# Scattering the gates of two steps at a time, with the low-gate one-hots scaled on ScalarE

## The chip, the cores and the metric

The kernel runs on one core of a Trainium2 chip. The metric is device time in microseconds (us), taken as the median of the timed runs. A profiled execution of the same program gives the traces that are quoted.

## What is computed

A trunk of two layers, 256 tokens of width 1024. Each layer has a token mixer (mLSTM in the first, RG-LRU in the second) with memory cross-attention, and then a PEER channel mixer. The change is in the PEER mixer:

```python
def peer_ffn(x, w_q, subkeys, u_tab, v_tab):      # PEER_EXPERTS = 128 * 128, 8 heads, top 16
    ...
        q = (xb @ w_q).reshape(n, PEER_HEADS, 2, PEER_HALF)
        s = jnp.einsum('nhpc,pkc->nhpk', q, sk)
        sv, si = lax.top_k(s, PEER_TOPK)
        cand = sv[:, :, 0, :, None] + sv[:, :, 1, None, :]
        cand_id = si[:, :, 0, :, None] * PEER_KEYS + si[:, :, 1, None, :]
        fv, fi = lax.top_k(cand.reshape(n, PEER_HEADS, PEER_TOPK * PEER_TOPK), PEER_TOPK)
        eid = ...                                  # the chosen experts, 8 * 16 = 128 for each token
        gw = jax.nn.softmax(fv, axis=-1)           # and their gates
        act = jax.nn.gelu(jnp.einsum('nhkd,nd->nhk', u_tab[eid], xb), approximate=False)
        return jnp.einsum('nhk,nhkd->nd', gw * act, v_tab[eid])
```

## The kernel before

The PEER mixer gathers nothing. It runs through all 128 x 128 experts in 128 blocks of 128, block i holding the experts whose number has one fixed second key. A step of the first half of the mixer computes `u @ x` for one block and all 256 tokens (`u_step`, 24 matmuls into one bank of the accumulator memory). The gates of the chosen experts are brought into the same layout, and products of gates and gelu values then weight the rows of `v` in the second half.

One core works in fp32 with each operand split into a high and a low part. For each block that is loaded (`next`, which calls `pump`), ScalarE casts the raw 128x1024 tile to the high part (L96), and VectorE and GpSimd subtract to get the low part. In the stage that the change touches, VectorE does columns 384 to 1023 (L104) and GpSimd the first 386 (L106); two columns are written by both, so that GpSimd starts behind VectorE. `u_step` of block i prepares block i + 2: three buffers (`HL_BUFS`) hold the two parts, so the cast for block i + 2 waits until TensorE is done with block i - 1. All engines execute their instructions in the order in which the program lists them.

A layer's `u` blocks are done in two stages. In the first (64 blocks, `lo`), VectorE also does the routing. In the second (63 blocks, `hi`; one more follows it), each step also scatters the gates of four tokens:

- `onehots(j)` builds, for the four tokens of step j, fp16 one-hot rows `oh`: VectorE compares an iota with the first and second key numbers (L878, 1024 elements a partition), then multiplies the first-key one-hots by the gates, which are held as a high and a low fp16 part (`gT`): both products are one instruction, L881, 1024 elements a partition, and the low product overwrites the one-hots it is made from.
- `scatter` is eight 128-column matmuls on TensorE (L1011) from `oh` into one bank: the gate of each expert for the four tokens.
- `finish(j)` applies gelu to the bank that `u_step(j)` left (`gated`: L911 and L913 on ScalarE, then the product L914 on VectorE), and brings the scattered gates in: a copy L902 on ScalarE, products L903 and L905 on VectorE.

The second stage lists, in step j: `u_step(j)`, `scatter` for step j, `finish(j - 1)`, `onehots(j + 1)`. `oh` has two buffers. [...]

Of the kernel before, what the change touches and what calls it, by code (L numbers as in the profile page):

```python
# [7 lines left out]
F32 = mybir.dt.float32  # L8
# [4 lines left out]
AF = mybir.ActivationFunctionType  # L13
ALU = mybir.AluOpType
# [3 lines left out]
P = 128  # L18
D = 1024
T = 256  # L20
# [23 lines left out]
class Trunk:  # L44
# [751 lines left out]
    def routing(self, w, tt):  # L796
        nc = self.nc
        sv, si, tmp = self.sv[tt], self.si[tt], self.tmp
        self.pool_cols = D
        sf = w.tile([P, 8, 2, 16], F16, name="sf")  # L800
        nc.vector.tensor_copy(sf, si)
        yield 0.4
        cand = w.tile([P, 8, NCAND], F32, name="cand")
        for n, (a0, na, nb, o) in enumerate(CAND):
            dv = cand[:, :, o:o + na * nb].rearrange("p h (a b) -> p h a b", a=na)
            i0 = sv[:, :, 0, a0:a0 + na].unsqueeze(3).to_broadcast([P, 8, na, nb])
            i1 = sv[:, :, 1, 0:nb].unsqueeze(2).to_broadcast([P, 8, na, nb])
            nc.vector.tensor_add(dv, i0, i1)
        yield 1.5
        fv = w.tile([P, 8, 16], F32, name="fv")  # L810
        fi = w.tile([P, 8, 16], U32, name="fidx")
        for h in range(0, 8, 2):
            yield from self.top16(*[(cand[:, h + p, :], fv[:, h + p, :], fi[:, h + p, :], tmp[:, p, :NCAND])
                                    for p in range(2)])
        self.pool_cols = 0
        gw = w.tile([P, 8, 16], F32, name="gw")
        gsum = w.tile([P, 8], F32, name="gsum")
        nc.vector.tensor_sub(gw, fv, fv[:, :, 0:1].to_broadcast([P, 8, 16]))
        nc.scalar.activation(gw, gw, AF.Exp)
        ff = w.tile([P, P], F16, name="ff")  # L820
        nc.vector.tensor_copy(ff, fi.rearrange("p a b -> p (a b)"))
        yield 0.6

        ge = w.tile([P, 2, 8, P], F16, name="ge")
        ab = w.tile([P, 2, P], F16, name="ab")
        over = w.tile([P, P], F16, name="over")
        nc.vector.tensor_tensor(ge[:, 0], self.edge, ff.unsqueeze(1).to_broadcast([P, 8, P]), op=ALU.is_le)
        nc.vector.tensor_scalar(over, ff, -float(TAIL0), 0.0, op0=ALU.add, op1=ALU.max)
        nc.vector.tensor_mul(ge[:, 1], ge[:, 0], self.wide)
        yield 1.7  # L830
        for n in (4, 2):
            nc.vector.tensor_add(ge[:, :, 0:n], ge[:, :, 0:n], ge[:, :, n:2 * n])
        nc.vector.tensor_add(ab, ge[:, :, 0], ge[:, :, 1])
        nc.vector.tensor_add(ab, ab, over.unsqueeze(1).to_broadcast([P, 2, P]))
        nc.vector.tensor_sub(ab[:, 1], ff, ab[:, 1])
        yield 1.9
        ef = w.tile([P, 2, P], F32, name="ef")
        for z in range(2):
            eq = w.tile([P, 8, 16, 16], F16, name="eq")
            full = [P, 8, 16, 16]  # L840
            nc.vector.tensor_tensor(eq, self.iotac.unsqueeze(1).to_broadcast(full),
                                    ab[:, z].rearrange("p (h k) -> p h k", h=8).unsqueeze(2).to_broadcast(full),
                                    op=ALU.is_equal)
            yield 1.25
            for hs in (slice(0, 4), slice(4, 8)):
                nc.vector.tensor_mul(eq[:, hs], eq[:, hs], sf[:, hs, z, :].unsqueeze(3).to_broadcast([P, 4, 16, 16]))
                yield 1.25
            for n in (8, 4, 2):
                nc.vector.tensor_add(eq[:, :, 0:n], eq[:, :, 0:n], eq[:, :, n:2 * n])
            nc.vector.tensor_add(ef[:, 1 - z].rearrange("p (h k) -> p h k", h=8), eq[:, :, 0], eq[:, :, 1])  # L850
            yield 1.8
        nc.vector.tensor_reduce(gsum, gw, axis=AX.X, op=ALU.add)
        nc.vector.reciprocal(gsum, gsum)
        nc.vector.tensor_mul(gw, gw, gsum.unsqueeze(2).to_broadcast([P, 8, 16]))
        yield 0.9

        def done():
            p = self.bank()
            n = P // 4
            js = slice(tt * n, (tt + 1) * n)  # L860
            steps = lambda a: a.rearrange("p (j t) -> p j t", t=4)
            nc.tensor.transpose(p[:, 0:P], ef[:, 0, :], self.ident)
            nc.tensor.transpose(p[:, P:2 * P], ef[:, 1, :], self.ident)
            nc.tensor.transpose(p[:, 2 * P:3 * P], gw.rearrange("p a b -> p (a b)"), self.ident)
            for z in range(2):
                nc.vector.tensor_copy(self.i12T[:, js, z], steps(p[:, z * P:(z + 1) * P]))
            gs = w.tile([P, n, 4], F32, name="gs")
            nc.vector.tensor_scalar(gs, steps(p[:, 2 * P:3 * P]), GSCALE, None, op0=ALU.mult)
            nc.vector.tensor_copy(self.gT[:, js, 0], gs)
            nc.vector.tensor_sub(self.gT[:, js, 1], gs, self.gT[:, js, 0])  # L870
        self.ready = done

    def onehots(self, j):
        nc = self.nc
        oh = self.ohp.tile([P, 3, 2, P, 2], F16, name="oh")
        pairs = lambda a: a.rearrange("p z (q t) -> p (z q) t", t=2).unsqueeze(2).to_broadcast([P, 4, P, 2])
        flat = lambda a: a.rearrange("p z q e t -> p (z q) e t")
        nc.vector.tensor_tensor(flat(oh[:, 1:3]), self.iota2.unsqueeze(1).to_broadcast([P, 4, P, 2]),  # L878
                                pairs(self.i12T[:, j]), op=ALU.is_equal)
        two = oh[:, 1].rearrange("p q e t -> p (q e t)").unsqueeze(1).to_broadcast([P, 2, 4 * P])  # L880
        nc.vector.tensor_tensor(flat(oh[:, 0:2]), two.rearrange("p z (q e t) -> p z q e t", q=2, t=2), pairs(self.gT[:, j]), op=ALU.mult)  # L881
        return oh

    def u_step(self):
# [31 lines left out]
    def peer_layer(self, layer):  # L916
        nc, tc, A = self.nc, self.tc, self.A
        with ExitStack() as ctx:
            wg = ctx.enter_context(tc.tile_pool(name=f"wglo{layer}", bufs=1))
            self.i12T = wg.tile([P, T // 4, 2, 4], F16, name="i12T")  # L920
            self.gT = wg.tile([P, T // 4, 2, 4], F16, name="gT")
            right = ctx.enter_context(ExitStack())
            lo = right.enter_context(tc.tile_pool(name=f"lo{layer}", bufs=1, side="right")).tile([P, N0, T], F32,
                                                                                               name="wglo")
            self.pool_cols = POOL_COLS
            with ExitStack() as rctx:
# [52 lines left out]
                for gq in range(2):  # L979
                    qb = self.proj_t(8, (self.xH, self.xL))  # L980
                    for b in range(4):
                        o = 8 * gq + 2 * b
# [8 lines left out]
                prev = None  # L991
                for i in range(N0 + 1):
                    g = self.u_step() if i < N0 else None
                    if prev is not None:
                        nc.scalar.activation(lo[:, i - 1, :], prev, AF.Gelu)
                    prev = g
                self.finish_sides()
            hi_p = ctx.enter_context(tc.tile_pool(name=f"wghi{layer}", bufs=1))
            hi = hi_p.tile([P, P - N0, T], F32, name="wghi")
            nj = P - N0  # L1000
            self.pool_cols, self.chained = HALF_COLS, True
            with ExitStack() as octx:
                self.ohp = octx.enter_context(tc.tile_pool(name=f"oh{layer}", bufs=2))
                oh = self.onehots(0)
                prev = None
                def scatter():
                    wp = self.bank()
                    for q in range(4):
                        qs = slice(q * P, (q + 1) * P)
                        for z in (0, 1):  # L1010
                            nc.tensor.matmul(wp[:, qs], oh[:, 2, q // 2, :, q % 2], oh[:, z, q // 2, :, q % 2], start=z == 0,  # L1011
                                             stop=z == 1, skip_group_check=True)
                    return wp
                for j in range(nj - 1):
                    g = self.u_step()
                    wp = scatter()
                    if prev is not None:
                        self.finish(lo, hi, j - 1, *prev)
                    if j == nj - 2:
                        oh = self.onehots(j + 1)  # L1020
                    prev = (g, wp)
                    if j < nj - 2:
                        oh = self.onehots(j + 1)
                wp = scatter()
                self.finish(lo, hi, nj - 2, *prev)
                self.finish(lo, hi, nj - 1, None, wp)
            cp = ctx.enter_context(tc.tile_pool(name=f"cp{layer}", bufs=HL_BUFS))
            cp.tile([P, GAP], F32, name="gap", bufs=1)
            self.pool_cols, self.chained = 0, False
# [7 lines left out]
            g = self.u_step()  # L1037
# [185 lines left out]
```

## Time and profile before

| | |
|---|---|
| median of three runs | 1867.91 us |
| lowest and highest | 1865.24 us, 1870.0 us |
| profiled execution, its own time | 1865.7 us |
| profiled execution, span | 1863.9 us |
| granted TensorE clock over the span | 0.99 |
| TensorE busy, VectorE busy, ScalarE busy, GpSimd busy | 98%, 70%, 50%, 23% |
| stage with the scatter, first to last scatter, first layer | 386.09 us to 589.82 us |
| matmuls and weight loads of the scatter | 1024 of each, in two layers |

In the rows below PE is TensorE's matmuls, PEld its weight loads, DVE VectorE, ACT ScalarE, POOL GpSimd. A row of the timeline holds the start and the duration in us, the engine, the source line, the operation, and what it writes and reads; brackets at the end hold the idle time of the engine before it and what ended that. A row of the groups holds the count, the busy time in us and the mean of one in ns. A busy TensorE is not one at its peak, since matmuls overlap: the distance between starts tells more than the durations.

### The profile page before, as it was taken

How to read it: one execution, taken by the hardware profiler on the slowest of the kernel's cores; microseconds unless marked ns; L12 is line 12 of the kernel's file. 1: busy time of each engine (PE TensorE's matmuls, PEld its weight loads, DVE VectorE, ACT ScalarE, POOL GpSimd, SP SyncE). 2: the span in 40 equal slices, each digit the busy share in tenths (PEclk: the TensorE clock that was granted, in tenths of full speed). 3: DMA queues.
4: the chain of work that ended last, by engine and by line, in shares of the span. 5: the costliest groups of instructions: out<-in, count | busy, mean ns of one | idle time of the engine just before them, and what ended most of it. 6: DMA issues, size and time to landing. Idle time of an engine off the chain costs nothing.

```text
span 1863.9 us, 33272 instructions
## 1 busy us (share of the span) xinstructions
PE 1821.8 (98%) x12770; PEld 1675.5 (90%) x12770; DVE 1298.0 (70%) x2665; ACT 940.3 (50%) x1604; POOL 428.7 (23%) x326
## 2 busy tenths in 40 slices
PE   8999999999999999999998899999999999999997
PEld 8898999999999888888887699999999988888886
DVE  6474579689998555666556638695999975555556
ACT  5454555455545444555537255554555454555543
POOL 2005772343331000000010258425333300000001
PEclk9999999999999999999999899999999999999999
DMA  7465556655555666667644166666555566666664
GB/s 244 132 178 171 179 177 191 199 174 161 165 163 162 196 195 193 193 215 227 205 169 139 59 193 177 198 192 192 160 161 165 162 179 193 193 193 194 193 194 132
DMA packets 94344, 333.42 MB, mean 179 GB/s; under 512 B 10600, under 2 KB 12904, under 8 KB 93928
## 3 DMA queue, kind: packets, MB, share of 16 engines
q1 hardware_dynamic: 93320, 328.66, 58.3%
q10 hardware_dynamic: 864, 2.62, 0.4%
q8 instruction: 100, 1.64, 0.4%
q14 instruction: 60, 0.49, 0.1%
HBM read 330.19 MB, written 1.05 MB: 178 GB/s over the span
## 4 chain that ended last, share of the span: by engine, by line
PE 72%; issue 15%; POOL 7%; DVE 3%; ACT 1%; DMA 1%; SPq 0%; POOLq 0%; ACTq 0%; DVEq 0%
PE bank L164 23%; PE bank L165 23%; PE bank L163 23%; POOL wL L106 7%; PE bank L222 3%; DVE wL L111 1%; DMA raw<-in_w0kg_dram 1%; ACT wH L96 0%; DMA raw<-in_w0qx_dram 0%; DVE xc L700 0%; PE bank L314 0%; DVE aa L747 0%; DVE x L293 0%; POOL wL L109 0%; DVE x L288 0%
## 5 line engine op out<-in xcount | busy, mean ns | idle before, releaser
L96 ACT CAST wH<-raw 128x1024 fp32r<-128x1024 f32 (+2 forms) x608 | 632.3, 1041 | 791.0 <-PE bank L165 330.2
L111 DVE TENSOR_TENSOR wL<-raw,wH 128x1024 fp32r<-128x1024 f32 (+3 forms) x413 | 468.5, 1137 | 455.7 <-ACT wH L96 455.1
L163 PE MATMUL bank<-xHL,wH 128*128 128x256 f32 x2536 | 717.6, 283 | 5.9 <-ACT wH L96 4.5
L165 PE MATMUL bank<-xHL,wL 128*128 128x256 f32 x2536 | 704.5, 278 | 7.3 <-DVE wL L111 7.3
L164 PE MATMUL bank<-xHL,wH 128*128 128x256 f32 x2536 | 704.5, 278 | 0.2
L165 PEld LDWEIGHTS bank<-xHL,wL 128*128 128x128 f32 x2536 | 479.1, 189 | 9.3 <-DVE wL L111 9.1
L163 PEld LDWEIGHTS bank<-xHL,wH 128*128 128x128 f32 x2536 | 479.1, 189 | 6.6 <-ACT wH L96 4.5
L164 PEld LDWEIGHTS bank<-xHL,wH 128*128 128x128 f32 x2536 | 479.6, 189 | 0.9 <-DVE xHL L219 0.9
L165 PE MATMUL bank<-wH,cL 128*128 128x512 f32 x1024 | 398.4, 389 | 0.0
L164 PE MATMUL bank<-wL,cH 128*128 128x512 f32 x1024 | 398.3, 389 | 0.0
L163 PE MATMUL bank<-wH,cH 128*128 128x512 f32 x1024 | 398.3, 389 | 0.0
L109 POOL TENSOR_TENSOR wL<-raw,wH 128x1024 fp32r<-128x1024 f32 (+1 forms) x121 | 258.1, 2136 | 211.7 <-ACT wH L96 181.1
L165 PEld LDWEIGHTS bank<-wH,cL 128*128 128x128 f32 x1024 | 192.2, 188 | 40.0
L163 PEld LDWEIGHTS bank<-wH,cH 128*128 128x128 f32 x1024 | 192.2, 188 | 39.9
L164 PEld LDWEIGHTS bank<-wL,cH 128*128 128x128 f32 x1024 | 192.2, 188 | 39.8
L106 POOL TENSOR_TENSOR wL<-raw,wH 128x386 fp32r<-128x386 f32 x126 | 129.7, 1029 | 279.9 <-DVE wL L104 279.9
L303 POOL TENSOR_TENSOR x<-x,raw 128x256 f32<-128x256 f32 x7 | 5.3, 760 | 614.4 <-ACT x L300 614.4
L878 DVE TENSOR_TENSOR oh<-iota,i12T 128x1024 f16<-128x1024 f16 x128 | 130.5, 1020 | 0.0
L104 DVE TENSOR_TENSOR wL<-raw,wH 128x640 fp32r<-128x640 f32 x126 | 104.0, 825 | 7.4
L881 DVE TENSOR_TENSOR oh<-oh,gT 128x1024 f16<-128x1024 f16 x128 | 90.1, 704 | 4.4
L1011 PE MATMUL bank<-oh 128*128 128x128 f16 x1024 | 81.1, 220 | 1.1 <-DVE oh L881 1.1
L1011 PEld LDWEIGHTS <-oh 128*128 128x128 f16 x1024 | 58.9, 98 | 6.0 <-DVE oh L881 1.5
(269 smaller groups left out, 1524.1 us busy)
## 6 DMA issues: line engine op xcount, KB each, us to landing
raw<-in_u_dram SPq DMA_DIRECT2D x256, 512.0 KB, 3.7
raw<-in_v_dram SPq DMA_DIRECT2D x256, 512.0 KB, 4.3
raw<-in_w_q_dram SPq DMA_DIRECT2D x32, 512.0 KB, 3.7
raw<-in_w_out_dram SPq DMA_DIRECT2D x16, 512.0 KB, 4.5
raw<-in_w0qx_dram SPq DMA_DIRECT2D x8, 512.0 KB, 4.7
raw<-in_wkv_dram SPq DMA_DIRECT2D x8, 512.0 KB, 4.7
raw<-in_w1x_dram SPq DMA_DIRECT2D x8, 512.0 KB, 4.4
raw<-in_w0v_dram SPq DMA_DIRECT2D x8, 384.0 KB, 3.7
```

The source lines that it names most:

```text
L96: (nc.vector.tensor_copy if self.cast_dve else nc.scalar.copy)(h[:, c], r[:, c])
L104: nc.vector.tensor_sub(l[:, k:], r[:, k:], h[:, k:].bitcast(F32))
L106: nc.gpsimd.tensor_sub(l[:, :k], r[:, :k], h[:, :k].bitcast(F32))
L109: nc.gpsimd.tensor_sub(l[:, :k], r[:, :k], h[:, :k].bitcast(F32))
L111: nc.vector.tensor_sub(l[:, k:], r[:, k:], h[:, k:].bitcast(F32))
L163: mm(out, sH, mH, start=start, stop=False, skip_group_check=True)
L164: mm(out, sH, mL, start=False, stop=False, skip_group_check=True)
L165: mm(out, sL, mH, start=False, stop=stop, skip_group_check=True)
L222: self.nc.tensor.matmul(out, lhsT, rhs, start=start, stop=stop, skip_group_check=True)
L878: nc.vector.tensor_tensor(flat(oh[:, 1:3]), self.iota2.unsqueeze(1).to_broadcast([P, 4, P, 2]), pairs(self.i12T[:, j]), op=ALU.is_equal)
L881: nc.vector.tensor_tensor(flat(oh[:, 0:2]), two.rearrange("p z (q e t) -> p z q e t", q=2, t=2), pairs(self.gT[:, j]), op=ALU.mult)
L1011: nc.tensor.matmul(wp[:, qs], oh[:, 2, q // 2, :, q % 2], oh[:, z, q // 2, :, q % 2], start=z == 0, stop=z == 1, skip_group_check=True)
```

## The change

Three things change. The steps are taken in pairs: after the `u_step` of an odd step, the gates of both steps are scattered, 16 matmuls in a row, so both buffers of `oh` are filled before TensorE reads either. The product with the low part of the gates leaves VectorE, whose L881 now makes the high product alone (512 elements a partition); ScalarE makes the low product in place, with four activations of 128 columns, one for each token, which take the gate as a per-partition scale from a new fp32 copy `gL` (one more VectorE copy for each half of the tokens). And `finish` moves behind `onehots`: step j lists `u_step(j)`, `onehots(j)`, `finish(j - 2)`, and, if j is odd, the two scatters.

```diff
+            nc.vector.tensor_copy(self.gL[:, js], self.gT[:, js, 1])
...
-        two = oh[:, 1].rearrange("p q e t -> p (q e t)").unsqueeze(1).to_broadcast([P, 2, 4 * P])
-        nc.vector.tensor_tensor(flat(oh[:, 0:2]), two.rearrange("p z (q e t) -> p z q e t", q=2, t=2), pairs(self.gT[:, j]), op=ALU.mult)
+        nc.vector.tensor_tensor(oh[:, 0], oh[:, 1],
+                                self.gT[:, j, 0].rearrange("p (q t) -> p q t", t=2).unsqueeze(2)
+                                .to_broadcast([P, 2, P, 2]), op=ALU.mult)
+        for q in range(4):
+            one = oh[:, 1, q // 2, :, q % 2]
+            nc.scalar.activation(one, one, AF.Identity, scale=self.gL[:, j, q:q + 1])
...
-                for j in range(nj - 1):
-                    g = self.u_step()
-                    wp = scatter()
-                    if prev is not None:
-                        self.finish(lo, hi, j - 1, *prev)
-                    if j == nj - 2:
-                        oh = self.onehots(j + 1)
-                    prev = (g, wp)
-                    if j < nj - 2:
-                        oh = self.onehots(j + 1)
-                wp = scatter()
-                self.finish(lo, hi, nj - 2, *prev)
-                self.finish(lo, hi, nj - 1, None, wp)
+                ohs, gs, done = [self.onehots(0)], [], []
+                for j in range(nj):
+                    gs.append(self.u_step() if j < nj - 1 else None)
+                    if j:
+                        ohs.append(self.onehots(j))
+                    if done:
+                        self.finish(lo, hi, j - 2, *done.pop(0))
+                    if j % 2:
+                        done = [(g, scatter(o)) for g, o in zip(gs, ohs)]
+                        ohs, gs = [], []
+                for j in (nj - 2, nj - 1):
+                    self.finish(lo, hi, j, *done.pop(0))
```

More of the change, by code (lines that the diff above doesn't have):

```diff
@@ L921, in peer_layer @@
             self.gT = wg.tile([P, T // 4, 2, 4], F16, name="gT")
+            self.gL = wg.tile([P, T // 4, 4], F32, name="gL")
             right = ctx.enter_context(ExitStack())
@@ L1003, in peer_layer, with scatter @@
                 self.ohp = octx.enter_context(tc.tile_pool(name=f"oh{layer}", bufs=2))
-                oh = self.onehots(0)
-                prev = None
-                def scatter():
+                def scatter(oh):
                     wp = self.bank()
@@ L1010, in scatter @@
                         for z in (0, 1):
-                            nc.tensor.matmul(wp[:, qs], oh[:, 2, q // 2, :, q % 2], oh[:, z, q // 2, :, q % 2], start=z == 0,
-                                             stop=z == 1, skip_group_check=True)
-                    return wp
-                for j in range(nj - 1):
-                    g = self.u_step()
-                    wp = scatter()
-                    if prev is not None:
-                        self.finish(lo, hi, j - 1, *prev)
-                    if j == nj - 2:
-                        oh = self.onehots(j + 1)
-                    prev = (g, wp)
-                    if j < nj - 2:
-                        oh = self.onehots(j + 1)
-                wp = scatter()
-                self.finish(lo, hi, nj - 2, *prev)
-                self.finish(lo, hi, nj - 1, None, wp)
+                            nc.tensor.matmul(wp[:, qs], oh[:, 2, q // 2, :, q % 2], oh[:, z, q // 2, :, q % 2],
+                                             start=z == 0, stop=z == 1, skip_group_check=True)
+                    return wp
+                ohs, gs, done = [self.onehots(0)], [], []
[10 more added lines that the diff above has]
+                    self.finish(lo, hi, j, *done.pop(0))
             cp = ctx.enter_context(tc.tile_pool(name=f"cp{layer}", bufs=HL_BUFS))
```

## The prediction

> **What bounds the kernel now.** I read the page first, then the table by stage, then the timeline of one round of the touched stage, engine by engine.
>
> ```profile
> span 1863.9 us, 33272 instructions
> PE 1821.8 (98%) x12770; PEld 1675.5 (90%) x12770; DVE 1298.0 (70%) x2665; ACT 940.3 (50%) x1604; POOL 428.7 (23%) x326
> ...
> 460.00:500.00 40.00, 40.00 (x394) 39.57 (x393) 38.80 (x76) 20.16 (x48) 13.00 (x13) 1.00 0.54 165
> ```
>
> The page says TensorE. The third row (length; busy time of PE, PEld, DVE, ACT, POOL; clock; DMA share) says that in this stage VectorE is nearly as full, 38.80 of 40 us, and ScalarE half empty. The timeline shows who waits.
>
> ```profile
> 471.02 0.63 PE L1011 MATMUL bank<-oh 128*128 128x128 f16 x8
> 471.46 0.37 PE L163 MATMUL bank<-xHL,wH 128*128 128x256 f32 x1
> 471.66 0.28 PE L164 MATMUL bank<-xHL,wH 128*128 128x256 f32 x1
> 471.78 0.28 PE L165 MATMUL bank<-xHL,wL 128*128 128x256 f32 x1
> ...
> 474.29 0.63 PE L1011 MATMUL bank<-oh 128*128 128x128 f16 x8
> ...
> 472.23 0.83 DVE L104 TENSOR_TENSOR wL<-raw,wH 128x640 fp32r<-128x640 f32 x1
> 472.97 0.26 DVE L914 TENSOR_TENSOR wghi<-wghi,bank 128x104 f32<-128x104 f32 x1
> 473.14 0.42 DVE L903 SCALAR_TENSOR_TENSOR wglo<-bank,wglo 128x256 f32<-128x256 f32 x1
> 473.48 0.26 DVE L905 SCALAR_TENSOR_TENSOR wghi<-bank,wghi 128x108 f32<-128x108 f32 x1
> 473.65 1.05 DVE L878 TENSOR_TENSOR oh<-iota,i12T 128x1024 f16<-128x1024 f16 x1
> 474.74 0.69 DVE L881 TENSOR_TENSOR oh<-oh,gT 128x1024 f16<-128x1024 f16 x1
> 475.50 0.83 DVE L104 TENSOR_TENSOR wL<-raw,wH 128x640 fp32r<-128x640 f32 x1
> ...
> 471.15 1.05 ACT L96 CAST wH<-raw 128x1024 fp32r<-128x1024 f32 x1 [1.54 <-POOL wL L106]
> 472.10 0.29 ACT L911 ACTIVATE wghi<-bank 128x152 f32<-128x152 f32 x1
> 472.42 0.24 ACT L913 ACTIVATE bank<-bank 128x104 f32<-128x104 f32 x1
> 472.58 0.29 ACT L902 ACTIVATE wghi<-bank 128x148 f32<-128x148 f32 x1
> 474.41 1.05 ACT L96 CAST wH<-raw 128x1024 fp32r<-128x1024 f32 x1 [1.55 <-POOL wL L106]
> ```
>
> A round takes 3.27 us on every engine (471.02 to 474.29; 472.23 to 475.50). TensorE has no idle time in it: the eight matmuls of the scatter and the switch back take 471.02 to 471.66, then matmuls follow every 0.11 us. VectorE is full to some 0.07 us, ScalarE has 1.5 us free. The important thing is how this fits: ScalarE's gelu work (L911 to L902) runs while VectorE is in L104, so L914 finds its input ready. The two engines work side by side, with a cast ahead of both.
>
> **The change, part by part.** The grouped scatter saves TensorE a switch: the first matmul behind a scatter is 0.20 us from its follower (471.46, 471.66) where 0.12 is usual, so about 0.1 us for every second step, 6 us in all if TensorE stays the bound.
>
> The product on VectorE halves; this is the row for a fp16 product of 512 elements. Its neighbour here changes too. In the old order three products on fp32 lay between L104 and L878; now L878 follows L104 at once, while GpSimd runs L106. The first round of the stage has that order already:
>
> ```profile
> L849 DVE TENSOR_TENSOR eq<-eq 128x512 f16<-128x512 f16 x8 | 3.4, 426 | 0.3
> ...
> 384.92 0.82 DVE L104 TENSOR_TENSOR wL<-raw,wH 128x640 fp32r<-128x640 f32 x1
> 385.67 0.68 DVE L878 TENSOR_TENSOR oh<-iota,i12T 128x1024 f16<-128x1024 f16 x1
> 386.38 1.39 DVE L881 TENSOR_TENSOR oh<-oh,gT 128x1024 f16<-128x1024 f16 x1
> ...
> 385.83 1.40 POOL L106 TENSOR_TENSOR wL<-raw,wH 128x386 fp32r<-128x386 f32 x1 [2.12 <-DVE wL L104]
> ```
>
> L106 stretches to 1.40 us and L881 from 0.69 to 1.39: fp16 work on VectorE and GpSimd's subtraction shut each other out, and L881 ends 0.54 us behind L106 (387.77, 387.23), that is 0.15 less than its length alone. With 0.43 instead of 0.69 the new product ends 0.28 behind, at 387.51, 1.84 us after L878 began. Without the collision it would be 0.71 + 0.43 = 1.14. I take 1.84, since the row is this very order; 1.14 stays as an end of the range. VectorE's one-hots thus take no less time than now (473.65 to 475.43, 1.78).
>
> The four products on ScalarE have no row of their own. The nearest are back-to-back activations with a per-partition scale, of 256 columns, and two casts for the price of a column:
>
> ```profile
> 1018.40 0.49 ACT L737 ACTIVATE th<-rr,n 128x256 f32<-128x256 f32 x1
> 1018.79 0.49 ACT L736 ACTIVATE aa<-rr,c 128x256 f32<-128x256 f32 x1
> ...
> L96 ACT CAST wH<-raw 128x1024 fp32r<-128x1024 f32 x574 | 604.1, 1054 | 756.1 <-PE bank L165 320.5 <-POOL wL L106 187.5 <-PE bank L164 122.6
> L218 ACT CAST cH<-wglo 128x256 fp32r<-128x256 f32 x128 | 51.5, 404 | 1.0 <-DVE wglo L903 1.0
> ...
> 751.06 1.05 ACT L96 CAST wH<-raw 128x1024 fp32r<-128x1024 f32 x1 [1.36 <-PE bank L165]
> ...
> 752.14 1.22 DVE L111 TENSOR_TENSOR wL<-raw,wH 128x1024 fp32r<-128x1024 f32 x1 [1.16 <-ACT wH L96]
> ```
>
> A column costs (1054 - 404) / 768 = 0.85 ns, 128 columns less are 0.11 us, so one takes 0.38 us and they start 0.39 - 0.11 = 0.28 to 0.30 apart, say 0.29: four hold ScalarE for 1.17 us. Ends: 0.64, at the 0.16 us between L913 and L902, which have no scale operand; 1.7, if each waits for the one before (0.38 + 0.04, four times). The last two rows give the 0.04 us by which VectorE starts behind a cast that it waits for (752.11, 752.14); I use it in both directions.
>
> The speed is not the trouble. The trouble is the queue. In each step ScalarE now lists cast, four products, L911, L913, L902. The products overwrite what the VectorE product reads, so they wait for it; gelu, the copy and the next cast are queued behind them; and VectorE's L914, L903 and L905, listed behind the one-hots, wait for gelu. What ran side by side becomes one chain, counted from the start of a cast:
>
> - cast and hand-over: 1.09 (751.06 to 752.14)
> - L104 until L878 starts: 0.75 (384.92 to 385.67), so 1.84
> - L878 and the product: 1.84, so 3.68, and 0.04 to ScalarE, 3.72
> - four products until L911 starts: 1.17, so 4.89
> - L911 to L913 0.32, to L902 0.16, to the next cast 0.19 (0.29 less the 0.10 by which a follower starts early, 471.15 + 1.05 against 472.10): 0.67, so 5.56.
>
> VectorE waits for gelu at 4.89 + 0.32 + 0.24 + 0.04 = 5.49, and its three products (0.17, 0.34, 0.17 between starts) end at 6.2; the next L104 comes at 5.56 + 1.09 = 6.65, so they are hidden. TensorE needs 48 matmuls and two scatters for two rounds, 2 x 3.27 - 0.1 = 6.44 us against 11.12: it now waits, 4.7 us in each pair, at the scatter for ScalarE's products. All its other demands are met earlier: a block is prepared two rounds ahead, and L878 of a new pair, which overwrites what the scatter reads, comes 2.4 us after the last product ended, the scatter some 1.1.
>
> Per layer: in the trace the first cast is at 383.84 us and the last scatter here:
>
> ```profile
> 383.84 1.05 ACT L96 CAST wH<-raw 128x1024 fp32r<-128x1024 f32 x1
> ...
> 589.82 0.63 PE L1011 MATMUL bank<-oh 128*128 128x128 f16 x8 [0.57 <-DVE oh L881]
> ```
>
> The products of step 0 push that cast to about 385.9; step 0 has no one-hots behind it (1.0) and step 1 no `finish` (5.0), so step 2 begins at 391.9. Then 61 rounds of 5.56 lead to 731.1, and step 63, without a cast, needs some 3.5 more to its scatter: 734.6, against 589.82, 144.8 later. Two layers: 290. On the profiled execution's own 1865.7 us (span 1863.9 and 1.8 around it) that is 2156; the median of the runs shown, 1867.91, lies 2.2 above it, so 2158.
>
> [...]
>
> **The rivals.**
>
> TensorE stays the bound (not slower). If the chain were under 3.2 us, the 0.1 us for each pair would be left: 63 x 0.1 = 6 less, 1862. It needs gelu to start ahead of the products, as if `finish` stood first in the queue; then VectorE would need 0.75 + 1.84 + 0.68 = 3.27, just on the edge. Against it: the orders L96, L911, L913, L902 and L104, L914, L903, L905, L878, L881 in the rows above are the program's, so nothing reorders. 4 in 100.
>
> The overlap is lost in part: the products come out near 0.64 and the collision is missed. 5.56 - 0.53 - 0.70 = 4.33, 122 rounds of 1.06 more, 1998. Each end alone gives 2093 and 2073. Between 1900 and 2070: 6 in 100.
>
> TensorE's clock drops in the 4.7 us pauses. The one long pause of the trace:
>
> ```profile
> 1023.41 6.74 PE L222 MATMUL bank<-pT,vm 128*128 128x256 f32 x16 [5.87 <-ACT pT L66]
> ...
> 1023.40:1025.00 1.60, 1.59 (x4) 1.32 (x5) 1.59 (x3) 0.44 (x1) 0.00 (x0) 0.50 0.00 0
> 1029.00:1031.00 2.00, 2.00 (x9) 1.59 (x9) 0.41 (x1) 0.80 (x2) 0.00 (x0) 0.86 0.00 0
> 1031.00:1036.00 5.00, 4.71 (x27) 3.93 (x25) 2.36 (x6) 2.44 (x2) 0.00 (x0) 1.00 0.00 0
> ```
>
> After 5.87 us the granted clock is 0.50, and back at 1.00 some 6.2 us into the work. The scatter and the first block of a pair (0.97 + 2.72) would then end 6.8 us after the pause, where the second cast of the pair could start at 6.1 (0.58 + 5.56): 0.7 late, 63 pairs, 44 us, 2202 if it happens in every pair. 8 in 100. [...]
>
> A table load for each change between gelu and the scaling.
>
> ```profile
> L995 ACT ACT_TABLE_LOAD x6 | 7.7, 1283 | 0.1
> ...
> L300 ACT ACTIVATE x<-x,nm,rs 128x256 f32<-128x256 f32 x3 | 1.8, 597 | 2.6 <-DVE nm L328 2.6
> ```
>
> At 1.28 us twice a round it would give about 2470. But the loads belong to functions such as gelu (L995); L300, the same function as the products, has a row for its activations and none for a load. 2 in 100.
>
> **How the numbers follow.** The serial chain at its own size has 80 in 100. Its bounds: 2073 without the collision, 2158 + 0.5 x 122 = 2219 with each product waiting for the one before, and 2232 for the clock (44) with two of those waits in four (30). So 2070 to 2230, forecast 2158. A measurement of this kernel tells 0.3% (5.6 us) from no change: slower 0.95, faster 0.04, within 0.01.
>
> **What would show it.** Casts 5.56 us apart in the stage, the first layer's last scatter near 735 us. TensorE about 58% busy there, waiting some 4.7 us in each pair at L1011 for ScalarE's products. VectorE waiting about 1.8 us a round at L914 for L913, and ScalarE about 2.6 us a round for VectorE's product. That product near 1.1 us and L106 at 1.40; the four products 0.38 us each and 0.29 apart. It is wrong if gelu stands ahead of the products in ScalarE's order, if casts stay 3.2 us apart, or if TensorE has no idle time there; the size is wrong if the product ends 1.1 us behind L878's start, or the products are 0.16 or 0.42 apart.

## The result, and the profile after

The changed kernel took 2156.12 us (median of five runs, 2155.01 to 2156.47) against 1866.88 us for the kernel before (five runs too, of which the table above has the first three), a ratio of 1.1546 (95% interval 1.1529 to 1.1563). The forecast was 2158, range 2070 to 2230. The profiled execution took 2156.47 us, 290.8 more than the one before.

The profile's page and the waits of the changed kernel. In the page's second row of digits stands the granted clock.

```profile
span 2154.7 us, 33848 instructions
...
PE 1957.7 (91%) x12770; PEld 1772.9 (82%) x12770; DVE 1326.8 (62%) x2669; ACT 1086.8 (50%) x2116; POOL 472.2 (22%) x326
...
PEclk9999999888888999999999999998888889999999
...
ACT oh L886 <- DVE oh L881: 314.4, 119, 3.5
DVE wghi L919 <- ACT bank L918: 223.5, 122, 1.9
...
PE bank L1015 <- DVE oh L881: 141.5, 65, 3.6
```

Two waits are new and face each other: ScalarE's products (L886) wait for VectorE's product (L881), 314 us in all, and VectorE's gelu product (now L919) waits for ScalarE's gelu (now L918), 224 us in 122 steps. TensorE, which had waited for VectorE's product at the scatter for 1.1 us in all (the row below is of the kernel before), waits there (now L1015) for 141.5 us.

```profile
L1011 PE MATMUL bank<-oh 128*128 128x128 f16 x1024 | 81.1, 220 | 1.1 <-DVE oh L881 1.1
```

One round in the timeline, by engine; the comparison L878 is now L879, the copy L902 now L907:

```profile
550.77 1.05 ACT L96 CAST wH<-raw 128x1024 fp32r<-128x1024 f32 x1
554.53 1.33 ACT L886 ACTIVATE oh<-oh,gL 128x128 f16<-128x128 f16 x4 [2.71 <-DVE oh L881]
555.71 0.27 ACT L916 ACTIVATE wghi<-bank 128x144 f32<-128x144 f32 x1
556.01 0.25 ACT L918 ACTIVATE bank<-bank 128x112 f32<-128x112 f32 x1
556.17 0.28 ACT L907 ACTIVATE wghi<-bank 128x140 f32<-128x140 f32 x1
556.34 1.05 ACT L96 CAST wH<-raw 128x1024 fp32r<-128x1024 f32 x1
...
561.83 1.05 ACT L96 CAST wH<-raw 128x1024 fp32r<-128x1024 f32 x1
...
551.85 0.82 DVE L104 TENSOR_TENSOR wL<-raw,wH 128x640 fp32r<-128x640 f32 x1 [0.32 <-ACT wH L96]
552.59 0.68 DVE L879 TENSOR_TENSOR oh<-iota,i12T 128x1024 f16<-128x1024 f16 x1
553.31 1.12 DVE L881 TENSOR_TENSOR oh<-oh,gT 128x512 f16<-128x512 f16 x1
556.29 0.27 DVE L919 TENSOR_TENSOR wghi<-wghi,bank 128x112 f32<-128x112 f32 x1 [1.86 <-ACT bank L918]
...
552.75 1.40 POOL L106 TENSOR_TENSOR wL<-raw,wH 128x386 fp32r<-128x386 f32 x1 [4.11 <-DVE wL L104]
```

The rows can be read as one chain without a gap: cast 550.77, L104 551.85, comparison 552.59, product 553.31 to 554.43, ScalarE's products 554.53, gelu 555.71 and 556.01, copy 556.17, the next cast 556.34. Rounds take 5.57 and 5.49 us in turn, 5.53 on average, where one took 3.27. Then TensorE, with the table by stage (length; busy time of PE, PEld, DVE, ACT, POOL; clock; DMA share):

```profile
557.39 0.63 PE L1015 MATMUL bank<-oh 128*128 128x128 f16 x8
560.04 0.29 PE L1015 MATMUL bank<-oh 128*128 128x128 f16 x1 [2.02 <-DVE oh L881]
560.51 1.14 PE L1015 MATMUL bank<-oh 128*128 128x128 f16 x7 [0.18 <-ACT oh L886]
...
384.00:736.00 352.00, 270.37 (x2042) 248.89 (x2041) 214.47 (x375) 179.13 (x508) 88.83 (x64) 0.86 0.32 98
```

The scatter of the even step goes out as soon as TensorE is done with the second block. That of the odd step starts 2.65 us later, when VectorE's product is there, and then goes at the pace of ScalarE's products. The 16 matmuls are not in a row, and the clock in the stage is 0.86.

### The profile page after: what moved, and what is told of

Its sections match the earlier page's. It is cut to its first block, busy times and chain, and to the rows that moved or that the text cites. A ratio compares the mean times of both kernels' runs of the same rounds, so it can differ in the third digit from the quotient of the medians.

```text
span 2154.7 us, 33848 instructions
## 1 busy us (share of the span) xinstructions
PE 1957.7 (91%) x12770; PEld 1772.9 (82%) x12770; DVE 1326.8 (62%) x2669; ACT 1086.8 (50%) x2116; POOL 472.2 (22%) x326
## 4 chain that ended last, share of the span: by engine, by line
PE 67%; DVE 17%; ACT 13%; issue 2%; DMA 1%; SPq 0%; ACTq 0%; DVEq 0%
PE bank L163 20%; PE bank L165 20%; PE bank L164 20%; DVE oh L881 6%; ACT oh L886 5%; ACT wH L96 5%; DVE wL L104 4%; DVE oh L879 3%; PE bank L222 3%; PE bank L1015 3%; ACT wghi L907 1%; ACT wghi L916 0%; DVE wL L111 0%; DMA raw<-in_w0kg_dram 0%; DMA raw<-in_w0qx_dram 0%
## 5 line engine op out<-in xcount | busy, mean ns | idle before, releaser
L163 PE MATMUL bank<-xHL,wH 128*128 128x256 f32 x2536 | 753.4, 297 | 5.8 <-ACT wH L96 4.4
L165 PE MATMUL bank<-xHL,wL 128*128 128x256 f32 x2536 | 740.5, 292 | 6.6 <-DVE wL L111 6.5
L164 PE MATMUL bank<-xHL,wH 128*128 128x256 f32 x2536 | 741.6, 292 | 0.2
L163 PEld LDWEIGHTS bank<-xHL,wH 128*128 128x128 f32 x2536 | 519.1, 205 | 13.6 <-ACT wH L96 4.4
L165 PEld LDWEIGHTS bank<-xHL,wL 128*128 128x128 f32 x2536 | 516.5, 204 | 8.0 <-DVE wL L111 7.8
L164 PEld LDWEIGHTS bank<-xHL,wH 128*128 128x128 f32 x2536 | 518.8, 205 | 0.8 <-DVE xHL L219 0.8
L886 ACT ACTIVATE oh<-oh,gL 128x128 f16<-128x128 f16 x512 | 168.8, 427 | 338.9 <-DVE oh L881 314.4
L106 POOL TENSOR_TENSOR wL<-raw,wH 128x386 fp32r<-128x386 f32 x126 | 174.0, 1381 | 513.5 <-DVE wL L104 513.5
L1015 PE MATMUL bank<-oh 128*128 128x128 f16 x1024 | 127.4, 234 | 158.1 <-DVE oh L881 141.5
L1015 PEld LDWEIGHTS <-oh 128*128 128x128 f16 x1024 | 71.9, 102 | 193.8 <-DVE oh L881 139.2
L919 DVE TENSOR_TENSOR wghi<-wghi,bank 128x4 f32<-128x4 f32 (+30 forms) x124 | 35.4, 285 | 223.5 <-ACT bank L918 223.5
L881 DVE TENSOR_TENSOR oh<-oh,gT 128x512 f16<-128x512 f16 x128 | 139.6, 1090 | 4.5
```

Source lines behind the costliest of these rows:

```text
L106: nc.gpsimd.tensor_sub(l[:, :k], r[:, :k], h[:, :k].bitcast(F32))
L163: mm(out, sH, mH, start=start, stop=False, skip_group_check=True)
L164: mm(out, sH, mL, start=False, stop=False, skip_group_check=True)
L165: mm(out, sL, mH, start=False, stop=stop, skip_group_check=True)
L881: nc.vector.tensor_tensor(oh[:, 0], oh[:, 1], self.gT[:, j, 0].rearrange("p (q t) -> p q t", t=2).unsqueeze(2) .to_broadcast([P, 2, P, 2]) ...
L886: nc.scalar.activation(one, one, AF.Identity, scale=self.gL[:, j, q:q + 1])
```

## The experiments

All are compared with the kernel before; its median lay at 1865.6 to 1866.9 us in the four groups of runs.

**1. The order of the queue.** `finish` ahead of `onehots`, nothing else.

```diff
+                    if done:
+                        self.finish(lo, hi, j - 2, *done.pop(0))
                     if j:
                         ohs.append(self.onehots(j))
-                    if done:
-                        self.finish(lo, hi, j - 2, *done.pop(0))
```

> The changed kernel with finish ahead of onehots in each step, nothing else. Theory of the chain: ScalarE's gelu work no longer waits for the products, but the next cast still does. The chain becomes cast and hand-over 1.09, L104 0.75, the three fp32 products 0.68, the comparison 1.05 and 0.03, the halved product 0.43, hand-over 0.07, four products 1.18: a round of 5.28 us where the changed kernel has 5.54, so 122 x 0.26 = 32 us less, near 2124. VectorE's wait for L918 is gone. Rival, the wait of VectorE for gelu is what costs: rounds fall to 3.3 us, near 1875.

Measured: 2121.43 us, ratio 1.1371 (1.1338 to 1.1404). ScalarE in one round:

```profile
547.52 1.03 ACT L96 CAST wH<-raw 128x1024 fp32r<-128x1024 f32 x1
548.46 0.27 ACT L916 ACTIVATE wghi<-bank 128x140 f32<-128x140 f32 x1
...
551.54 1.32 ACT L886 ACTIVATE oh<-oh,gL 128x128 f16<-128x128 f16 x4 [2.33 <-DVE oh L881]
552.73 1.03 ACT L96 CAST wH<-raw 128x1024 fp32r<-128x1024 f32 x1
```

Gelu is back beside VectorE's L104, but the cast still stands behind the products: 5.21 us a round. The late gelu carries some 33 us of the loss (289 against 256 above the kernel before), the late cast, by this reading, most of the rest; run 6 tests that.

**2. The pairs without ScalarE's products.** The one L881 of the kernel before, pairs and late `finish` as in the changed kernel.

```diff
-        nc.vector.tensor_tensor(oh[:, 0], oh[:, 1], ...)
-        for q in range(4): ...
+        two = oh[:, 1].rearrange("p q e t -> p (q e t)").unsqueeze(1).to_broadcast([P, 2, 4 * P])
+        nc.vector.tensor_tensor(flat(oh[:, 0:2]), two.rearrange("p z (q e t) -> p z q e t", q=2, t=2), pairs(self.gT[:, j]), op=ALU.mult)
```

> The changed kernel with both products of the gates on VectorE in one instruction, as before; the pairs and the late finish stay. Theory of the chain: ScalarE waits for VectorE at no place, the two engines run side by side again, and VectorE alone sets the round: 0.75 + 0.71 + 1.36 (full product, held up by GpSimd) + 0.68 = 3.50 us against 3.27, so about 28 us above the kernel before, near 1897. Rival, pairing makes TensorE wait for two sets of one-hots and carries most of the loss: above 2000.

Measured: 1927.97 us, ratio 1.0334 (1.0304 to 1.0364): neither number. Two rounds of VectorE, then the scatter on TensorE, the last matmul of the block behind it, and a cast:

```profile
470.44 0.83 DVE L104 TENSOR_TENSOR wL<-raw,wH 128x640 fp32r<-128x640 f32 x1 [0.59 <-ACT wH L96]
471.90 1.39 DVE L882 TENSOR_TENSOR oh<-oh,gT 128x1024 f16<-128x1024 f16 x1
...
477.90 0.83 DVE L104 TENSOR_TENSOR wL<-raw,wH 128x640 fp32r<-128x640 f32 x1 [0.56 <-ACT wH L96]
...
473.35 0.63 PE L1011 MATMUL bank<-oh 128*128 128x128 f16 x8 [0.65 <-DVE oh L882]
...
476.58 0.28 PE L165 MATMUL bank<-xHL,wL 128*128 128x256 f32 x1
...
476.82 1.05 ACT L96 CAST wH<-raw 128x1024 fp32r<-128x1024 f32 x1 [2.91 <-POOL wL L106]
```

The part that I had left out is a loop through TensorE, once in a pair: the odd step's one-hots are made in the step that scatters them, so the scatter waits for them (473.35), the next block starts behind it, the cast for the odd step waits until that block is done (last matmul 476.58, cast 476.82; the bracket names the L106 of GpSimd, but its row, 474.74 and 1.40 long, ends at 476.14), and L104 and the one-hots wait for that cast. A pair takes 7.46 us here, 3.73 a round. VectorE's own work in it is 3.45 us a round, near the 3.50 expected; the rest is its wait for that cast, 0.56 us in a pair. Pairs and late order cost 62 us without any product on ScalarE. They do not add to the longer chain: with the products on ScalarE and gelu ahead of them, the pairs (run 1) stand 256 us above the kernel before and single steps (run 3) 253.

**3. ScalarE's products without the pairs.** The kernel before, with the new L881 and the four activations in `onehots`.

```diff
-        nc.vector.tensor_tensor(flat(oh[:, 0:2]), two.rearrange(...), pairs(self.gT[:, j]), op=ALU.mult)
+        nc.vector.tensor_tensor(oh[:, 0], oh[:, 1], self.gT[:, j, 0]..., op=ALU.mult)
+        for q in range(4):
+            one = oh[:, 1, q // 2, :, q % 2]
+            nc.scalar.activation(one, one, AF.Identity, scale=self.gL[:, j, q:q + 1])
```

> The kernel before with the four products on ScalarE alone: a scatter in every step and finish ahead of onehots, as before. Theory of the chain: the next cast stands behind the products, which wait for VectorE, whose work waits for the cast: 5.28 us a round as in the run with finish first, 124 x 2.01 = 249 us more than before, near 2117. Rival, the loss needs the pairs: near 1867, or a little less since VectorE has 0.27 us less to do.

Measured: 2118.35 us, ratio 1.1354 (1.1321 to 1.1387).

```profile
548.62 1.32 ACT L886 ACTIVATE oh<-oh,gL 128x128 f16<-128x128 f16 x4 [2.34 <-DVE oh L881]
549.81 1.03 ACT L96 CAST wH<-raw 128x1024 fp32r<-128x1024 f32 x1
...
555.03 1.03 ACT L96 CAST wH<-raw 128x1024 fp32r<-128x1024 f32 x1
```

As expected, the cast stands behind the products and a round takes 5.22 us: the products alone, at that place, bring 253 us, where the whole change brings 289. The mean granted clock was 0.986 here, so the loss does not need a lowered clock either.

**4. The collision with GpSimd.** The changed kernel with `pool_cols` 0 in the stage: VectorE subtracts all columns.

```diff
-            self.pool_cols, self.chained = HALF_COLS, True
+            self.pool_cols, self.chained = 0, True
```

> The changed kernel with GpSimd out of the stage: VectorE subtracts all 1024 columns. Theory, the product of 512 elements takes 1.1 us only because GpSimd runs beside it: L104 costs 0.40 more (1.15 to its follower), the product falls to 0.43, 0.70 less: rounds of 5.26 us, 34 us less than the changed kernel, near 2122. Rival, the product is slow by its own access pattern: it stays at 1.1, rounds of 5.9 us, near 2200.

Measured: 2118.94 us, ratio 1.1357 (1.1324 to 1.139).

```profile
551.07 1.23 DVE L111 TENSOR_TENSOR wL<-raw,wH 128x1024 fp32r<-128x1024 f32 x1 [0.32 <-ACT wH L96]
552.21 0.69 DVE L879 TENSOR_TENSOR oh<-iota,i12T 128x1024 f16<-128x1024 f16 x1
552.93 0.43 DVE L881 TENSOR_TENSOR oh<-oh,gT 128x512 f16<-128x512 f16 x1
```

Without GpSimd beside it the product takes 0.43 us instead of 1.12. VectorE's longer subtraction costs less than the collision did: the kernel is 253 us above the one before, not 289.

**5. TensorE's clock.** The changed kernel with filler in TensorE's pause.

```diff
+WARM = 64
...
-                def scatter(oh):
+                def scatter(oh, warm):
                     wp = self.bank()
+                    for _ in range(warm):
+                        nc.tensor.matmul(wp[:, :P], self.iota2[:, :, 0], self.iota2[:, :, 1], start=True, stop=True,
+                                         skip_group_check=True)
...
-                        done = [(g, scatter(o)) for g, o in zip(gs, ohs)]
+                        done = [(g, scatter(o, WARM * z)) for z, (g, o) in enumerate(zip(gs, ohs))]
```

> The changed kernel with 64 matmuls of 128 columns ahead of the scatter of each odd step, in the pause of TensorE (they write the bank that the scatter then overwrites; 64 x 0.055 = 3.5 us of the 4.6 that TensorE has free in a pair at full clock). Theory of the chain: TensorE's clock, 0.86 in the stage, costs nothing, since two blocks and two scatters fit into a pair even at the lower clock: the clock comes back to 0.97 or more and the time stays within 5 us of 2156. Rival, the lowered clock is part of the loss: 20 to 45 us less, near 2120.

Measured: 2156.77 us, ratio 1.1556 (1.1537 to 1.1576). Table by stage, for most of the first layer's stage:

```profile
400.00:720.00 320.00, 314.79 (x3711) 299.93 (x3710) 194.60 (x347) 164.08 (x463) 79.77 (x58) 1.00 0.33 97
```

The clock is 1.00 and the time is the same: the lowered clock was a symptom.

**6. The products where their input is a step old.** `onehots` makes the VectorE part only; a function `scaled` makes the four activations. Against run 3, the products move from ahead of the next cast to behind it and behind gelu.

```diff
+                    if done:
+                        self.finish(lo, hi, j - 1, *done)
+                    self.scaled(j, ohs[0])
+                    done = (gs.pop(0), scatter(ohs.pop(0)))
+                    if j < nj - 1:
+                        ohs.append(self.onehots(j + 1))
```

> ScalarE's products put where their input is a step old: step j lists u_step(j), finish(j-1), the four products for step j, the scatter of step j, and VectorE's one-hots for step j+1. No pairs. Theory of the chain: nothing on ScalarE waits for VectorE any more; ScalarE needs 1.05 + 0.6 + 1.2 = 2.85 us a round, VectorE 0.75 + 0.68 + 1.05 + 0.46 = 2.95, both under TensorE's 3.27, and the products end 2.85 us behind the start of the cast where TensorE comes to the scatter at 3.04: the time of the kernel before, 1867, within 3. Rival, ScalarE's products are too dear in themselves or slow the other engines: 50 us or more above it.

Measured: 1867.91 us, ratio 1.0011 (1.0002 to 1.002).

```profile
473.33 1.05 ACT L96 CAST wH<-raw 128x1024 fp32r<-128x1024 f32 x1 [0.34 <-POOL wL L106]
474.28 0.29 ACT L918 ACTIVATE wghi<-bank 128x152 f32<-128x152 f32 x1
...
474.94 1.31 ACT L889 ACTIVATE oh<-oh,gL 128x128 f16<-128x128 f16 x4
476.60 1.05 ACT L96 CAST wH<-raw 128x1024 fp32r<-128x1024 f32 x1 [0.35 <-POOL wL L106]
```

The same four products, as long as in the changed kernel, and the round is 3.27 us. ScalarE goes through its queue without a wait for VectorE and has 0.34 us left. In run 3 they wait 2.34 us. So nearly all of run 3's 253 us is a matter of the place in the queue; run 7 puts the pairs back. Nothing is gained, since TensorE sets the round.

**7 to 9. The pairs on top of that.** Two scatters behind the odd step need a third buffer of one-hots, and room for it came from one of the five raw tiles. Run 8 is the kernel before with four raw tiles, run 9 is run 7 with the scatter in each step.

```diff
-RAW_BUFS, HL_BUFS = 5, 3
+RAW_BUFS, HL_BUFS = 4, 3
...
-                self.ohp = octx.enter_context(tc.tile_pool(name=f"oh{layer}", bufs=2))
+                self.ohp = octx.enter_context(tc.tile_pool(name=f"oh{layer}", bufs=3))
...
                     if done:
-                        self.finish(lo, hi, j - 1, *done)
+                        self.finish(lo, hi, j - 2, *done.pop(0))
-                    self.scaled(j, ohs[0])
-                    done = (gs.pop(0), scatter(ohs.pop(0)))
+                    self.scaled(j, ohs[-1])
+                    if j % 2:
+                        done = [(g, scatter(o)) for g, o in zip(gs, ohs)]
+                        ohs, gs = [], []
```

> The same with the scatter in pairs behind the odd step, which needs three buffers of one-hots; the raw tiles fall from five to four to make room. Theory: TensorE stays the bound and saves one switch of 0.1 us in each pair: 63 x 0.1 = 6 us under the kernel before, near 1860, if four raw tiles do. Rival, TensorE waits for the products of the odd step, since two scatters come 0.4 us earlier in it: 1867 or a little above.

> The kernel before with four raw tiles in place of five, the control for the run with deferred pairs. A tile lands 3.7 to 4.3 us after its issue and a block is taken every 2.7 to 3.3 us: no change expected, within 3 us of 1867; if the fifth tile matters, some 10 us above.

> The run with deferred pairs, with the scatter in each step instead of in pairs, and its three buffers and four raw tiles kept: all that is left of the difference is pairing. With pairs the matmuls of u_step started every 0.118 us in the stage, 0.114 without (0.004 x 48 x 63 = 11 us). Theory, pairing itself is what slows them: back to 0.114, and some 6 us less than the 1876 of the pairs, near 1870 as with four raw tiles alone. Rival, the third buffer or the four raw tiles move the addresses and slow them: 0.118, and 1876 or more.

Measured: 1875.97 (1.0055, 1.0043 to 1.0067) with the pairs, 1869.64 (1.0017, 1.0009 to 1.0026) with four raw tiles alone, 1870.42 (1.0023, 1.0014 to 1.0033) with all but the pairs. So pairing, in a kernel where TensorE waits 0.4 us in all for the products, costs 5.6 us between runs 9 and 7 (6 by their ratios) instead of saving 6. Two scatters of run 7:

```profile
464.96 1.09 PE L1017 MATMUL bank<-oh 128*128 128x128 f16 x16
471.60 1.09 PE L1017 MATMUL bank<-oh 128*128 128x128 f16 x16
```

A pair takes 6.64 us, where two rounds of run 9 take 6.53 (scatters at 464.33 and 470.86). The starts in the timeline from 450 to 474 us show where that comes from: `u_step`'s matmuls came every 0.1176 us with pairs, 0.1141 in run 9, and 0.1139 in the kernel before.

**10. A run of 16 short matmuls.** The kernel before with each scatter issued twice in a row (the second writes the same values again).

```diff
-                    for q in range(4):
+                    for q in (0, 1, 2, 3, 0, 1, 2, 3):
```

> The kernel before with each step's scatter issued twice, 16 matmuls in a row into the same bank with the same result. Theory, a run of 16 short matmuls slows the u_step matmuls behind it: these start 0.118 us apart in the stage, and a round grows by 0.44 + 24 x 0.004 = 0.54 us, 68 us in all. Rival, it is the 48 matmuls without a scatter between them, or the order of the banks: 0.114 as before, 0.44 us a round, 56 us.

Measured: 1933.24 us, 67.1 above the kernel before (ratio 1.0357, 1.0338 to 1.0375).

```profile
470.79 1.09 PE L1011 MATMUL bank<-oh 128*128 128x128 f16 x16
471.69 0.36 PE L163 MATMUL bank<-xHL,wH 128*128 128x256 f32 x1
471.89 0.28 PE L164 MATMUL bank<-xHL,wH 128*128 128x256 f32 x1
...
474.48 0.28 PE L165 MATMUL bank<-xHL,wL 128*128 128x256 f32 x1
474.60 0.58 PE L1011 MATMUL bank<-oh 128*128 128x128 f16 x7
```

From 471.89 there are 23 intervals to 474.60: 0.1178 us each, with no pairs, no third buffer of one-hots and all five raw tiles. The first theory holds: 16 short matmuls in a row are enough. Why they slow the long ones behind them stays open.

## Why the prediction was right

The chain is what bounds the stage, and its terms came out as worked: cast and hand-over 1.08 (1.09 forecast), L104 0.74 (0.75), comparison and product 1.84 (1.84), the four products 1.18 (1.17), gelu and copy 0.63 (0.67). Only the hand-over to ScalarE was 0.10 and 0.04 in turn, not 0.04. Together 5.53 us a round where 5.56 was forecast. The last scatter of the first layer was forecast near 734.6 us; its odd part began at 733.88:

```profile
733.88 0.22 PE L1015 MATMUL bank<-oh 128*128 128x128 f16 x1 [2.35 <-DVE oh L881]
```

The changed kernel and runs 1, 3, 7 and 6 have the same products and stand 289, 256, 253, 9 and 1 us above the kernel before. In the first three the products wait for VectorE with the next cast queued behind them, in the changed kernel with gelu too; in the last two their input is a step old. Run 7 has the pairs, run 6 has not. Run 4 confirms the collision term, 0.43 against 1.12 us.

Five steps were off, none of which moved the sum:

- **TensorE's pause.** I had it wait 4.7 us in each pair with both scatters behind it. The even scatter goes early and the odd one starts with VectorE's product, so the wait is some 2 us. TensorE is 77% busy in the stage (270 of 352 us), not 58%: part of the time it runs at a granted clock of 0.50 (560.07 to 563.48 in the pair above), and the odd scatter takes 1.61 us (560.04 to 561.65) where eight matmuls otherwise take 0.63.
- **The clock.** I gave a drop in every pair 8 in 100, going by the one pause of 5.87 us in the trace. In the first layer's stage it fell 25 times in the 32 pairs, for 3.41 or 6.83 us at a time, though TensorE's waits at the scatter are 2.2 us on average (141.5 us in 65). Run 5 shows that it cost nothing: the first block of the pair still ended in time, at 554.6, with the cast behind it at 556.34. The rival's price was too high, for it took the clock to stay low through 6.2 us of work in every pair, and 20 of the 25 drops lasted 3.41. A frequent drop at no price was not worked out beforehand: that it left the time alone is luck. And the pause need not be near 5.87 us: the drop at 560.07 came behind 2.0 us without a matmul, and in the 3.41 us ahead of it TensorE was busy for 1.39 (rows in the last section).
- **The gain of the pairs.** The 0.1 us saved at the switch is real (one start 0.20 us behind the last in a pair of run 7, two in two rounds of run 9), but the 48 matmuls of the pair pay 0.0037 us each for it, 0.18 us. By runs 7 and 9, the rival in which TensorE stays the bound would have ended some 6 us slower, not 6 us faster.
- **The loop through TensorE** (run 2). I had said that all of TensorE's other demands are met earlier. That holds only as long as ScalarE's chain is the longer one.
- **The length of one product.** I had 0.38 us from the casts; the 512 products took 427 ns on average. They start 0.295 us apart, where I took 0.29 out of a span of 0.28 to 0.30, and the chain counts that distance alone.

ScalarE is slower at these fp16 products, by a ratio of about 2.7: the four hold it for 1.18 us, and VectorE's product of as many elements takes 0.43 in run 4. But that is not what cost the time: run 6 has the slow ScalarE products and loses 1 us.

## What to carry to other kernels

Work moved to a half-idle engine has to be priced at its place in that engine's queue, not by its length: ask what is listed behind it, and who waits for that. Before moving it, list its input's producer: if that is the engine which waits for what stands behind it, two engines that ran side by side become one chain. The cure is then to issue the moved work one step later than its input, which here took the loss from 253 to 1 us without the pairs (runs 3 and 6), and from 289 to 9 with them (run 7).

## What the runs showed of the hardware that I had not expected

Behind 16 matmuls of 128 fp16 columns in a row, the 256-column matmuls start 0.118 us apart up to the next scatter (runs 7 and 10, from 450 to 474 us in the first layer and from 1400 to 1424 us in the second). Behind a run of eight they start 0.1139 us apart in the kernel before, and 0.1133 without any short ones (the first stage, from 330 to 348 us). The granted clock was 1.00 in the stage of run 7 and in both stretches of the kernel before, and 0.991 over all of run 10. Run 2, where a wait breaks the 16 into two eights, has both, each for a whole pair: 0.118 behind the scatter that begins at 472.06 us, 0.114 behind the one at 457.21. So the run need not be unbroken, and 16 in a pair do not always do it.

And the granted clock fell to 0.50 behind a pause of 2.0 us. The table by stage shows when one drop began and ended; the two matmuls below it, behind the odd scatter of the pair before, start 0.21 us apart, nearly twice the usual distance:

```profile
558.00:560.00 2.00, 0.03 (x1) 0.00 (x0) 1.95 (x3) 0.00 (x0) 1.38 (x1) 1.00 0.00 0
560.00:560.20 0.20, 0.16 (x1) 0.13 (x2) 0.00 (x0) 0.18 (x1) 0.00 (x0) 0.68 0.00 0
560.20:563.40 3.20, 3.02 (x17) 2.63 (x16) 1.30 (x4) 2.64 (x8) 0.00 (x0) 0.50 0.54 164
563.40:563.60 0.20, 0.20 (x3) 0.20 (x2) 0.20 (x1) 0.00 (x0) 0.00 (x0) 0.79 0.00 0
...
551.14 0.41 PE L163 MATMUL bank<-xHL,wH 128*128 128x256 f32 x1
551.35 0.41 PE L164 MATMUL bank<-xHL,wH 128*128 128x256 f32 x1
```

A mean of 0.68 over 0.20 us, between 1.00 and 0.50, puts the drop at 560.07, and 0.79 puts the return at 563.48: 3.41 us at half clock. The drop came as the odd scatter began, behind 2.0 us without a matmul. The pair before has its drop from 549.83 to 553.24, again 3.41 us, and the two drops are 10.24 us apart, three times that, while the pairs are 11.06 apart. Worked out in the same way from stretches of 0.2 us, each of the 25 drops of the stage starts three to seven times 3.41 us behind the one before. Why some pairs had none was not shown. And the clock fell with TensorE busy for 0.97 to 1.87 us of the 3.41 before each drop, 1.39 before the one at 560.07.
